# A hybrid attention layer in fp32: other first loads, an order by parts for the first products, two weight splits moved, and the last squares on another engine

## The chip, the cores and the metric

The kernel runs on one core of a Trainium2 chip. The core has five engines with queues of their own: TensorE (PE; its weight loads are listed apart as PEld), VectorE (DVE), ScalarE (ACT), GpSimd (POOL) and SyncE (SP), the last of which only starts transfers here. Engines wait for each other through semaphores; each works through its own queue in order. The time is that of one execution on the device in microseconds, 766.73 as the median of three runs before the change (765.64, 766.73, 766.76).

## The reference

One layer of a trunk on 512 frames of width 1024, with 256 memory tokens, all in float32:

```python
hn = rmsnorm(h, norm_mix_g[l])
proj = hn @ w_in[l]
fq, fk, fv, ff, gq, gf, gi, gg = jnp.split(proj, split_idx, axis=-1)
fox_out = fox_attention(to_heads(fq), to_heads(fk), to_heads(fv), log_f)   # causal softmax, 8 heads of 64
rec = hgrn2_chunkwise(gq, gf, gi, lbs[l])                                  # gated recurrence, 4 heads of 128
rec = rmsnorm(rec, hgrn_norm_g[l]) * silu(gg)
h = h + concatenate([fox_out, rec]) @ w_out[l]
h = h + memory_cross_attention(rmsnorm(h, norm_x_g[l]), rmsnorm(mem, norm_mem_g[l]), w_xq, w_xkv, w_xo)
u = rmsnorm(h, norm_ff_g[l]) @ w1[l]
h = h + square(relu(u)) @ w2[l]                                            # d_ff = 4096
return rmsnorm(h, final_norm_g)
```

The softmax adds to each score the difference of two running sums of log forget gates. The factor of the first RMSNorm depends on the row alone, so the kernel multiplies by it behind the projection.

## The kernel before

**Products.** TensorE computes with operands of a reduced float format (fp32r). Every fp32 operand is split into a high part (a rounding copy) and a low part (what is left), and a product is three: high by high, high by low, low by high. For activations the high part of the normalised x is `hn_hi` and the low part `hn_lo`; for weights they are `wh` and `wl`. `gemm_fm` (L225) runs over the eight chunks of 128 inputs and issues for each chunk the three products L232 (wh by hi), L233 (wh by lo), L234 (wl by hi) of 128x512 elements into one PSUM bank. L245 to L247 are the same for 264 columns.

**Weights.** Panels of 256 columns are loaded on SyncE's queue into raw tiles (`wr`, two halves a and b per panel), and split by `split_of` (L164): ScalarE copies the high part (L167), VectorE subtracts for the low part (L169). `next_panel` (L204) loads and splits one panel ahead of the one in use. Panel 0 comes in quarters (`load_next(4)`), 256 KB each. Panel 11 is the first one of the memory's value projection.

**Order.** TensorE's instructions stand in the order in which the program records them; ScalarE and VectorE are in recorded order only up to the end of the first products. Elsewhere a scheduler sets their order by priorities (`ahead`), and `issue_after` and `keep_in_program_order` bind single instructions. SyncE's queue only starts transfers.

**Stages,** in us of the span: to 23 the loads of x, its transposes (`x_T`, L402, names `xt` and `xn`; four per chunk c) and the first two row blocks of the first panel, products `gf`; to 57 more projections and gates; 57 to 67 the diagonal blocks of the recurrence (`dg`, L611, four heads, 16 products of 64 columns each), with pieces of the projection `gi` between them as fill (`fill.run(F1)`, L614); to 120 the levels of the recurrence; to 150 its state chain; to 270 the softmax attention; to 440 the output projection and the cross attention; then the MLP, and from 755 the last RMSNorm.

**Softmax attention.** 32 units (p, tb, j): head pair, block of 128 queries, head in the pair. For each unit the scores (L881, L882), the mask and maximum on VectorE (L887), the exponential on ScalarE (L889), the scaling (L890, L891), four or fewer transposes into a PSUM slot `pt` (L899) and a copy of these (`ptb`, `pta`; L910 on ScalarE for j = 0, L912 on VectorE for j = 1). Fill runs between: projections `pq` and `pk`, and transposes `mnt` of the memory (L362), whose results are taken by `meh` (ScalarE, L364) and `mel` (VectorE, L365). `mnt` and `pt` share PSUM slots.

**MLP.** Each product of weights by activations is done on 2x2 blocks with seven products instead of eight; an up unit ("u", g, name) multiplies a 512 KB weight block by sums of the input's quarters, a down unit ("d", ...) multiplies by sums of the squared hidden values. `unit` (L1320) prepares splits of coming weight blocks (`prep`, L1308; whu and wlu up, whd and wld down) up to four ahead. Results of up units stand in PSUM banks `uU` and `uY`; `h` (L1398) is a copy held for a later unit, `c` (L1405) adds it, `hb` (L1434, L1436) are the split sums for the down units.

**End.** `squares` (L1513) takes the square of the finished columns on ScalarE with their running sum, adds the sums of the pieces (`fe`, L1521); GpSimd raises them to the power -1/2 (L1544), and both ScalarE and VectorE scale and store the rows.

Of the kernel before, what the change touches and what calls it, by code (L numbers as in the profile page):

```python
# [9 lines left out]
F32 = mybir.dt.float32  # L10
R = mybir.dt.float32r
U8 = mybir.dt.uint8
AF = mybir.ActivationFunctionType
# [29 lines left out]
def emit(  # L43
# [110 lines left out]
    stream = []  # L154
    state = {"used": 0, "then": None}
    UW, UK = WT + FH, KC // 2
# [16 lines left out]
    def load_unit(name, spec, ks, parts=1, between=None):  # L173

        nw = max(sl.stop for sl, _ in spec)
        hi, lo = new_parts([UK, nw], name)
        raw_ = wrp.tile([P, UK * nw], F32, tag="wr", name=f"wr{name}", padded_shape=[P, UK * UW])
        raw_ = raw_.rearrange("p (k n) -> p k n", k=UK)
        nk = UK // parts
        splits = []  # L180
        for q in range(parts):
            qs, src_ks = slice(q * nk, (q + 1) * nk), slice(ks.start + q * nk, ks.start + (q + 1) * nk)
            for sl, src in spec:
                nc.sync.dma_start(raw_[:, qs, sl], src[:, src_ks, :])
            if between is not None:
                between(q)
            splits.append(split_of(hi[:, qs, :], lo[:, qs, :], raw_[:, qs, :]))
        return (hi, lo), splits
# [15 lines left out]
    def next_panel():  # L204
        while len(stream) < min(state["used"] + 2, len(specs)):
            for split in load_next():
                with ahead(PW), ExitStack() as order:
                    for ins in last_copy[-2:] if len(stream) == 10 else ():
                        order.enter_context(tc.issue_after(ins))
                    split()  # L210
        if state["used"] == len(specs) - 1:
            state["then"]()
        r = stream[state["used"]]
        state["used"] += 1
        return r
# [8 lines left out]

    def gemm_fm(ps, wt, col, ahi, alo, n=S, order=range(KC)):  # L225

        whi, wlo = wt
        sl = slice(col, col + P)
        for n_, k in enumerate(order):
            hi, lo = chunk(ahi, k, slice(0, n)), chunk(alo, k, slice(0, n))  # L230
            wh, wl = chunk(whi, k, sl), chunk(wlo, k, sl)
            te.matmul(ps, wh, hi, start=n_ == 0, stop=False)  # L232
            te.matmul(ps, wh, lo, start=False, stop=False)  # L233
            te.matmul(ps, wl, hi, start=False, stop=n_ == KC - 1)  # L234
            yield 3 * n / 2400
# [73 lines left out]
    def load_x(g, n=WT, queue=ac):  # L309
        gs = slice(g, g + n)  # L310
        queue.dma_start(xt[:, :, gs], x[:, gs].rearrange("(t p) n -> p t n", p=P))

    load_x(0, P, nc.sync)
    load_x(P, P)
    for q in range(1, 3):
        load_x(q * WT)
    first = load_next(4)
    load_x(3 * WT, queue=nc.sync)
    rows = t2("rows", F32, (P,))[0:33, :]
# [12 lines left out]
    ve.memset(mhalf, -0.5)  # L332
    ones = cp.tile([P, 1], F32, name="ones")
    ve.memset(ones, 1.0)

# [99 lines left out]
    with tc.manual_schedule(engines={mybir.EngineType.Activation, mybir.EngineType.DVE}):  # L435
# [10 lines left out]
        gfps = [mm(f"gf{i}") for i in range(2)]  # L446
        gfg = [gemm_fm(gfps[i], wt0, i * P, hn_hi, hn_lo) for i in range(2)]
        second = []
# [24 lines left out]
        for c in range(KC):  # L473
            for g in gfg:
                next(g)
# [127 lines left out]
    for hp in range(2):  # L603
        Ac.append(t2(f"Ac{hp}", F32, (8, 64)))
        for j in range(2):
# [7 lines left out]
            gp.tensor_tensor(qt_(h), qt_(h), Fg[hp][:, j, :], op=ALU.mult)  # L613
            fill.run(F1)  # L614

# [247 lines left out]
    units = [(p, tb, j) for p in range(4) for tb in range(NT) for j in range(2)]  # L863
    prob, probT, held_T = {}, {}, {}

# [9 lines left out]
    def fox_scores(u):  # L875
# [7 lines left out]
        with ahead(P3):  # L883
# [4 lines left out]
            den = sm(1, f"dn{h}{tb}")  # L888
            ac.activation(b, b, AF.Exp, bias=mx, scale=-1.0, accum_out=den)  # L889
            ve.reciprocal(den, den)  # L890
            ve.tensor_scalar(b, b, den, None, op0=ALU.mult)  # L891

    def fox_T(u):
# [10 lines left out]
        with ahead(P4):  # L904
            if tb == NT - 1:
                probT[u] = t2(f"pts{h}{tb}")
            else:
                probT[u] = held_T[p, tb % 2][:, j, (0 if tb else 3 * P) :][:, 0:n]
            if j == 0:
                ac.activation(probT[u], pt[:, 0:n], AF.Copy)  # L910
# [26 lines left out]
    for n in range(len(units) + LAG):  # L937
        if n < len(units):
# [19 lines left out]
            if n == 2:  # L958
                fill.until("fv0")
            if n + 1 < len(units):  # L960
                fox_bias(units[n + 1])
# [319 lines left out]

    last_sum = {}

# [24 lines left out]
    def prep(kind, g, name):  # L1308
# [4 lines left out]
        unit_ = new_parts([k, D // k], f"{kind}{g}{name}")  # L1313
        with ahead(PW):
            split_of(unit_[0], unit_[1], raw.rearrange("p (k n) -> p k n", k=k))()
# [4 lines left out]
    def unit(*key):  # L1320
# [4 lines left out]
        kept = sum(k in units and keys.index(k) < keys.index(key) for k in last_keys)  # L1325
        while unit_q and kept + sum(k in units for k in keys[keys.index(key) :]) < 4:
            prep(*unit_q.popleft())
# [100 lines left out]
    def hidden_part(g, name):  # L1428
# [4 lines left out]
        sign = -1.0 if name == "6" else 1.0  # L1433
        ac.activation(hb[:, 0], src, AF.Copy, scale=sign)  # L1434
        if name == "6":
# [77 lines left out]
    def squares(tb, cs, last=False):  # L1513
        n = len(sums.setdefault(tb, []))
        ms = sm(1, f"fm{tb}{n}")
        if tb not in outs:
            outs[tb] = k4([D], f"fo{tb}")
        ac.activation(outs[tb][:, cs], acc[tb][:, cs], AF.Square, scale=1.0 / 32.0, accum_out=ms)
        if n:
            e = sm(1, f"fe{tb}{n}")  # L1520
            (ve if last else gp).tensor_scalar(e, ms, sums[tb][-1], EPS if last else 0.0, op0=ALU.add, op1=ALU.add)  # L1521
            ms = e
# [102 lines left out]
```

## Time and profile before

| What | Value |
|---|---|
| median of three runs | 766.73 us (765.64 to 766.76) |
| profiled execution | 765.97 us, span 763.9 us (2.07 us lie around the span) |
| TensorE busy | 751.6 us (98% of the span) |
| VectorE, ScalarE, GpSimd busy | 559.7, 427.1, 182.9 us |
| waits of TensorE that the profile names | 5.0 us in five places |

The span runs from the first to the last recorded instruction; the run's time is a little longer, and 0.76 us less than the median. A row of the timeline has the start and the duration in us, the engine, the line in the kernel, the operation with output<-input, the shape, and in brackets the idle time of the engine before it with what ended that. A product's recorded duration is longer than its share of the engine, since products overlap; the distance from one start to the next tells what it costs. The profile lists the granted clock of TensorE (PEclk, 1.00 is full).

### The profile page before, as it was taken

To read this page: it belongs to the slowest core of one execution; us is meant where nothing else is said; L and a number is where in the kernel's file an instruction comes from. 1 tells how busy PE (TensorE), PEld (TensorE's weight loads), DVE (VectorE), ACT (ScalarE), POOL (GpSimd) and SP (SyncE) were. 2 spreads that over 40 slices of the span, in tenths; PEclk is the share of its full clock that TensorE was granted. 3 is DMA by queue.
4 is the path that set the end of the run, shared out by engine and by line. 5 is a ranking of instruction groups with operands and counts; after the bars stand their busy time and mean duration, and the time that the engine had idled before them with its cause. 6 is when DMAs were issued, how large, how long until landed. Compare 5 with 4: busy or idle time off the path is not lost.

```text
span 763.9 us, 12648 instructions
## 1 busy us (share of the span) xinstructions
PE 751.6 (98%) x4844; PEld 665.8 (87%) x4844; DVE 559.7 (73%) x889; ACT 427.1 (56%) x718; POOL 182.9 (24%) x261
## 2 busy tenths in 40 slices
PE   8999999999999999999999999999999999999996
PEld 5889878978989988888888898999999999999985
DVE  4746766797677746645557789869797979897984
ACT  4655555676656533334445576656565757565743
POOL 7106343444343005510000111211212121211122
PEclk9999999999999999999999999999999999999998
DMA  7643322243444443221124498896979797978612
GB/s 225 216 114 86 111 82 57 84 111 85 142 161 137 131 150 111 87 79 56 56 83 137 83 295 171 231 253 161 249 165 241 183 268 164 280 148 213 161 47 110
DMA packets 84221, 113.08 MB, mean 148 GB/s; under 512 B 4881, under 2 KB 62778, under 8 KB 84162
## 3 DMA queue, kind: packets, MB, share of 16 engines
q1 hardware_dynamic: 70418, 74.77, 30.9%
q0 software_dynamic: 11568, 35.15, 22.6%
q10 hardware_dynamic: 2176, 2.36, 0.9%
q8 instruction: 38, 0.62, 0.3%
q14 instruction: 21, 0.17, 0.1%
HBM read 88.14 MB, written 4.21 MB: 121 GB/s over the span
## 4 chain that ended last, share of the span: by engine, by line
PE 90%; DVE 3%; DMA 2%; ACT 2%; issue 1%; POOL 1%; POOLq 0%; ACTq 0%; SPq 0%; DVEq 0%
PE uU L1394 4%; PE uU L1393 4%; PE uU L1395 4%; PE U L1495 3%; PE U L1496 3%; PE U L1497 3%; PE uY L1393 3%; PE uY L1395 3%; PE uY L1394 3%; PE xq L232 2%; PE xq L233 2%; PE xw L232 2%; PE xw L234 2%; PE xw L233 2%; PE xq L234 2%; PE wo L233 2%
## 5 line engine op out<-in xcount | busy, mean ns | idle before, releaser
L167 ACT ACTIVATE whd<-wq 128x1024 fp32r<-128x1024 f32 x39 | 41.3, 1058 | 31.3 <-PE U L1497 12.9
L169 DVE TENSOR_TENSOR wld<-wq,whd 128x1024 fp32r<-128x1024 f32 x39 | 47.6, 1220 | 7.1 <-ACT whd L167 7.1
L167 ACT ACTIVATE whu<-uq 128x1024 fp32r<-128x1024 f32 x28 | 29.7, 1062 | 33.0 <-PE uY L1394 14.3
L1395 PE MATMUL uU<-x2s,wlu 128*128 128x256 f32 x160 | 45.3, 283 | 0.0
L1393 PE MATMUL uU<-x2s,whu 128*128 128x256 f32 x160 | 45.2, 283 | 0.0
L1495 PE MATMUL U<-whd,hb 128*128 128x512 f32 x112 | 43.9, 392 | 0.0
L1496 PE MATMUL U<-wld,hb 128*128 128x512 f32 x112 | 43.9, 392 | 0.0
L1497 PE MATMUL U<-whd,hb 128*128 128x512 f32 x112 | 43.6, 389 | 0.0
L1250 POOL DMA_DIRECT2D uk<-us x8 | 7.2, 906 | 149.6 <-ACT acc L1114 85.7
L1467 DVE SCALAR_TENSOR_TENSOR acc<-U,r,acc 128x512 f32<-128x512 f32 x56 | 40.2, 744 | 1.8 <-PE U L1497 1.2
L169 DVE TENSOR_TENSOR wlu<-uq,whu 128x1024 fp32r<-128x1024 f32 x28 | 34.2, 1221 | 5.7 <-ACT whu L167 5.4
L1394 PE MATMUL uU<-x2a,whu 128*128 128x256 f32 x128 | 36.2, 283 | 0.0
L1394 PE MATMUL uY<-x2a,whu 128*128 128x256 f32 x128 | 36.2, 283 | 0.0
L1394 PE MATMUL uU<-x2b,whu 128*128 128x256 f32 x128 | 36.2, 283 | 0.0
L167 ACT ACTIVATE whu<-us 128x1024 fp32r<-128x1024 f32 x20 | 21.2, 1062 | 21.6 <-PE uU L1394 17.9
L169 DVE TENSOR_TENSOR wlu<-us,whu 128x1024 fp32r<-128x1024 f32 x20 | 24.4, 1221 | 10.8 <-ACT whu L167 10.8
L1393 PEld LDWEIGHTS uU<-x2s,whu 128*128 128x128 f32 x160 | 30.6, 191 | 0.8
L1395 PEld LDWEIGHTS uU<-x2s,wlu 128*128 128x128 f32 x160 | 30.6, 191 | 0.0
L889 ACT ACTIVATE bi<-bi,mx 128x128 f32<-128x128 f32 (+3 forms) x32 | 18.0, 561 | 20.5 <-DVE mx L887 20.2
L1250 POOL DMA_DIRECT2D wq<-in_w_dram x10 | 12.2, 1221 | 71.6 <-DMA wq<-in_w_dram 60.9
L872 POOL TENSOR_SCALAR bi<-nF,Ft 128x128 f32<-128x128 f32 (+3 forms) x32 | 21.5, 673 | 31.1 <-PE pt L899 17.1
L1393 PE MATMUL uY<-x2s,whu 128*128 128x256 f32 x96 | 27.3, 284 | 1.0 <-DVE c L1405 1.0
(961 smaller groups left out, 2809.1 us busy)
## 6 DMA issues: line engine op xcount, KB each, us to landing
wq<-in_w_dram SPq DMA_DIRECT2D x31, 512.0 KB, 6.0
uq<-in_w_dram SPq DMA_DIRECT2D x12, 512.0 KB, 4.7
us<-in_w_dram SPq DMA_DIRECT2D x12, 512.0 KB, 6.8
wq<-wq POOLq DMA_DIRECT2D x11, 512.0 KB, 6.4
wq<-in_w_dram POOLq DMA_DIRECT2D x10, 512.0 KB, 9.0
uk<-in_w_dram SPq DMA_DIRECT2D x8, 512.0 KB, 4.1
uk<-us POOLq DMA_DIRECT2D x8, 512.0 KB, 4.5
uq<-uk POOLq DMA_DIRECT2D x8, 512.0 KB, 6.1
```

The lines of the kernel that those rows point to most:

```text
L167: ac.activation(hi, raw, AF.Copy)
L169: ve.tensor_tensor(lo, raw, f(hi), ALU.subtract)
L232: te.matmul(ps, wh, hi, start=n_ == 0, stop=False)
L233: te.matmul(ps, wh, lo, start=False, stop=False)
L234: te.matmul(ps, wl, hi, start=False, stop=n_ == KC - 1)
L1393: te.matmul(ps[:, i, :], whi[:, k, ws], xh, start=first_ and (k, i) == (0, 0), stop=False, skip_group_check=True)
L1394: te.matmul(ps[:, i, :], whi[:, k, ws], xl, start=False, stop=False, skip_group_check=True)
L1395: te.matmul(ps[:, i, :], wlo[:, k, ws], xh, start=False, stop=k == 3, skip_group_check=True)
L1467: ve.scalar_tensor_tensor(a, ps, r2[:, 0 if sign > 0 else 1, tb : tb + 1], a, op0=ALU.mult, op1=ALU.add)
L1495: te.matmul(ps, hi, whi[:, k, :], start=first_ and k == 0, stop=False, skip_group_check=True)
L1496: te.matmul(ps, hi, wlo[:, k, :], start=False, stop=False, skip_group_check=True)
L1497: te.matmul(ps, lo, whi[:, k, :], start=False, stop=k == 1, skip_group_check=True)
```

## The change

Seven edits:

1. x's first three wide pieces no longer go out together on ScalarE's queue, nor the four weight quarters at once on SyncE's: SyncE's queue now has them in turn, x behind w. A copy of a constant into one column of x's tile, on ScalarE, stands before the first wide piece of x, which is held until the copy is done.
2. The six products of the first chunk are ordered by parts (both high by high, both low weight, both low activation) instead of by row block.
3. The fill between the diagonal blocks runs twice as long after each second block, and not at all after each first one.
4. The split of panel 11's second half (wh11b, wl11b) is issued behind the exponential and the scaling of the fourth softmax unit.
5. For the first head pair, all copies of `pt` are on ScalarE.
6. In the MLP, the split of up unit (1, "6") is issued behind the cast hb of unit (0, "6"), and at one step there is room for three prepared units, not four.
7. The squares of the very last 128x256 piece and their sum are one reduction on VectorE that starts from the running sum, and EPS is added one step earlier.

```diff
@@ load_unit
-                nc.sync.dma_start(raw_[:, qs, sl], src[:, src_ks, :])
+                load = nc.sync.dma_start(raw_[:, qs, sl], src[:, src_ks, :])
+                if between is not None:
+                    tc.keep_in_program_order(load)
@@ next_panel
-            for split in load_next():
+            for half, split in enumerate(load_next()):
...
-                    split()
+                    if (len(stream), half) == (12, 1):
+                        later.append(split)
+                    else:
+                        split()
@@ gemm_fm: begun=False added; the chunks' start and stop follow from it and from len(order)
@@ first loads
+    ones = cp.tile([P, 1], F32, name="ones")
+    ve.memset(ones, 1.0)
     load_x(0, P, nc.sync)
     load_x(P, P)
-    for q in range(1, 3):
-        load_x(q * WT)
-    first = load_next(4)
-    load_x(3 * WT, queue=nc.sync)
+    tc.keep_in_program_order(ac.activation(xt[:, 0, WT : WT + 1], ones, AF.Copy))
+
+    def x_behind(part):
+        if part < 3:
+            tc.keep_in_program_order(load_x((part + 1) * WT, queue=nc.sync))
+
+    first = load_next(4, x_behind)
@@ first chunk
-        gfg = [gemm_fm(gfps[i], wt0, i * P, hn_hi, hn_lo) for i in range(2)]
+        for part in ("hh", "lh", "hl"):
+            for i, ps in enumerate(gfps):
+                w, a = (wt0["hl".index(part[0])][0][:, 0, i * P : (i + 1) * P], (hn_hi, hn_lo)["hl".index(part[1])][:, 0, :])
+                te.matmul(ps, w, a, start=part == "hh", stop=False)
+        gfg = [gemm_fm(gfps[i], wt0, i * P, hn_hi, hn_lo, order=range(1, KC), begun=True) for i in range(2)]
@@ diagonal blocks
-            fill.run(F1)
+        fill.run(2 * F1)
@@ fox_scores
-            ac.activation(b, b, AF.Exp, bias=mx, scale=-1.0, accum_out=den)
+            exp = ac.activation(b, b, AF.Exp, bias=mx, scale=-1.0, accum_out=den)
             ve.reciprocal(den, den)
-            ve.tensor_scalar(b, b, den, None, op0=ALU.mult)
+            ends[u] = exp.ins, ve.tensor_scalar(b, b, den, None, op0=ALU.mult).ins
@@ fox_T
-            if j == 0:
+            if j == 0 or p == 0:
@@ the attention's loop
+            if n == 4:
+                with ahead(PW), tc.issue_after(ends[units[3]][0]), tc.issue_after(ends[units[3]][1]):
+                    later.pop()()
@@ prep
-        with ahead(PW):
+        with ahead(PW), tc.issue_after(hb_ins[0, "6"]) if (kind, g, name) == ("u", 1, "6") else nullcontext():
@@ unit
-        while unit_q and kept + sum(k in units for k in keys[keys.index(key) :]) < 4:
+        room = 3 if key == ("u", 1, "2") else 4
+        while unit_q and kept + sum(k in units for k in keys[keys.index(key) :]) < room:
@@ hidden_part
-        ac.activation(hb[:, 0], src, AF.Copy, scale=sign)
+        hb_ins[g, name] = ac.activation(hb[:, 0], src, AF.Copy, scale=sign).ins
@@ squares
+        if last and tb == NT - 1:
+            a = acc[tb][:, cs]
+            tc.keep_in_program_order(ve.tensor_tensor_reduce(out=outs[tb][:, cs], in0=a, in1=a, scale=1.0 / D, scalar=sums[tb][-1], op0=ALU.mult, op1=ALU.add, accum_out=ms))
+            sums[tb].append(ms)
+            return
...
-            (ve if last else gp).tensor_scalar(e, ms, sums[tb][-1], EPS if last else 0.0, op0=ALU.add, op1=ALU.add)
+            (ve if last else gp).tensor_scalar(e, ms, sums[tb][-1], EPS if last or tb == NT - 1 else 0.0, op0=ALU.add, op1=ALU.add)
```

What this does to the order of three queues is shown below; line numbers behind the first edits are higher in the changed kernel.

SyncE's queue at the start of the program, before (`xt` is x's tile, in pieces of 128 or 256 columns; `wr0a` and `wr0b` are panel 0's halves, in quarters; `rows` are small vectors of gains):

```order
L311 DMA xt<-in_x_dram 128x4x128
L184 DMA wr0a<-in_w_in_dram 128x2x256 x2
L184 DMA wr0b<-in_w_in_dram 128x2x256 x2
L311 DMA xt<-in_x_dram 128x4x256
L321 DMA rows<-in_norm_x_g_dram 8x128
```

And with the change:

```order
L316 DMA xt<-in_x_dram 128x4x128
L184 DMA wr0a<-in_w_in_dram 128x2x256
L331 DMA rows<-in_norm_x_g_dram 8x128
L331 DMA rows<-in_norm_mem_g_dram 8x128
L331 DMA rows<-in_norm_ff_g_dram 8x128
L316 DMA xt<-in_x_dram 128x4x256
L184 DMA wr0a<-in_w_in_dram 128x2x256
L316 DMA xt<-in_x_dram 128x4x256
L184 DMA wr0b<-in_w_in_dram 128x2x256
L316 DMA xt<-in_x_dram 128x4x256
L184 DMA wr0b<-in_w_in_dram 128x2x256
```

The two wide pieces of x that were ScalarE's are SyncE's now, each wide piece stands ahead of the weight quarter that is used with it, and three small loads have moved ahead of all of them.

VectorE in the attention, before, around the second unit (L887 is mask and maximum, L890 and L891 the scaling of the first unit, `mel` the low part of the memory's chunk):

```order
L169 TENSOR_TENSOR wl11a<-wr11a,wh11a 128x1024
L890 RECIPROCAL dn_1737<-dn_1737 128x1
L891 TENSOR_SCALAR bi_1661<-bi_1661,dn_1737 128x128
L169 TENSOR_TENSOR wl11b<-wr11b,wh11b 128x1024
L887 ISA bi_1727,mx_1783<-ps_1780,bi_1727 128x128
L887 ISA mx_1783 128x1
L365 SCALAR_TENSOR_TENSOR mel_1791<-mnt_1793,gv,meh_1789 128x256
```

ScalarE with the change, where wh11b now stands (`meh` of two memory chunks, `ptb` the copies of the third and fourth unit, L901 the exponential of the fifth):

```order
L372 ACTIVATE meh_1789<-mnt_1882,gv 128x256
L167 ACTIVATE wh11b<-wr11b 128x1024
L922 ACTIVATE ptb_1893<-pt_1890 128x256
L167 ACTIVATE wh12a<-wr12a 128x1024
L901 ACTIVATE bi_1851,dn_1907<-bi_1851,mx_1905 128x384
L372 ACTIVATE meh_1789<-mnt_1914,gv 128x256
L922 ACTIVATE ptb_1893<-pt_1925 128x256
```

On VectorE, wl11b has left its place behind L891 and stands behind the fifth unit's maximum, directly ahead of wl12a; the last copy above was VectorE's.

ScalarE in the MLP, before (`whu` and `whd` are high parts of up and down weights, `h` the held copy, `hb` the casts of hidden sums `n_0` and `s_0`):

```order
L1434 ACTIVATE hb_4982<-sq_4715 128x512
L167 ACTIVATE whu_5013<-uq_4597 128x1024
L167 ACTIVATE whu_5045<-uq_4596 128x1024
L1434 ACTIVATE hb_5010<-n_0_5007 128x512
L1398 ACTIVATE h_5043<-uU_5018 128x512
L1434 ACTIVATE hb_5101<-s_0_5006 128x512
L167 ACTIVATE whd_5079<-wq 128x1024
```

And with the change:

```order
L1450 ACTIVATE hb_4983<-sq_4716 128x512
L167 ACTIVATE whu_5014<-uq_4598 128x1024
L1414 ACTIVATE h_5044<-uU_5019 128x512
L1450 ACTIVATE hb_5011<-n_0_5008 128x512
L1450 ACTIVATE hb_5102<-s_0_5007 128x512
L167 ACTIVATE whu_5075<-uq_4597 128x1024
L167 ACTIVATE whd_5080<-wq 128x1024
```

The second whu has moved behind h and both casts; h stands ahead of the casts. On VectorE the low part of the same weight moves behind `c` in the same way.

More of the change, by code (lines that the diff above doesn't have):

```diff
@@ L154, in emit @@
     stream = []
-    state = {"used": 0, "then": None}
+    state, later = {"used": 0, "then": None}, []
     UW, UK = WT + FH, KC // 2
@@ L221, in chunk, with gemm_fm @@
         return t[:, k, sl]
-    def gemm_fm(ps, wt, col, ahi, alo, n=S, order=range(KC)):
+    def gemm_fm(ps, wt, col, ahi, alo, n=S, order=range(KC), begun=False):
         whi, wlo = wt
@@ L231, in gemm_fm @@
             wh, wl = chunk(whi, k, sl), chunk(wlo, k, sl)
-            te.matmul(ps, wh, hi, start=n_ == 0, stop=False)
+            te.matmul(ps, wh, hi, start=n_ == 0 and not begun, stop=False)
             te.matmul(ps, wh, lo, start=False, stop=False)
-            te.matmul(ps, wl, hi, start=False, stop=n_ == KC - 1)
+            te.matmul(ps, wl, hi, start=False, stop=n_ == len(order) - 1)
             yield 3 * n / 2400
@@ L310, in load_x @@
         gs = slice(g, g + n)
-        queue.dma_start(xt[:, :, gs], x[:, gs].rearrange("(t p) n -> p t n", p=P))
+        return queue.dma_start(xt[:, :, gs], x[:, gs].rearrange("(t p) n -> p t n", p=P))
+    ones = cp.tile([P, 1], F32, name="ones")
+    ve.memset(ones, 1.0)
     load_x(0, P, nc.sync)
     load_x(P, P)
-    for q in range(1, 3):
-        load_x(q * WT)
-    first = load_next(4)
-    load_x(3 * WT, queue=nc.sync)
+    tc.keep_in_program_order(ac.activation(xt[:, 0, WT : WT + 1], ones, AF.Copy))
[3 more added lines that the diff above has]
+    first = load_next(4, x_behind)
     rows = t2("rows", F32, (P,))[0:33, :]
@@ L332, in emit @@
     ve.memset(mhalf, -0.5)
-    ones = cp.tile([P, 1], F32, name="ones")
-    ve.memset(ones, 1.0)
     def rstd_of(ms, n, name, r=None):
@@ L473, in emit @@
         for c in range(KC):
-            for g in gfg:
+            for g in gfg if c else ():
                 next(g)
@@ L863, in emit @@
     units = [(p, tb, j) for p in range(4) for tb in range(NT) for j in range(2)]
-    prob, probT, held_T = {}, {}, {}
+    prob, probT, held_T, ends = {}, {}, {}, {}
     def fox_bias(u):
@@ L1280, in begin @@
             first_sums(kind, 0)
-    last_sum = {}
+    last_sum, hb_ins = {}, {}
     def behind(kind, g, name):
```

## The prediction

> **What bounds the kernel now.** I read the page's head and busy times first, then TensorE's waits, then the clock and the timeline at each place that the diff touches.
>
> ```profile
> span 763.9 us, 12648 instructions
> ...
> PE 751.6 (98%) x4844; PEld 665.8 (87%) x4844; DVE 559.7 (73%) x889; ACT 427.1 (56%) x718; POOL 182.9 (24%) x261
> ```
>
> TensorE (PE) is busy in 98% of the span; no other engine comes near. A gain can only be time in which PE stands still or is slow, or time behind its last product. The waits of PE say where it stands still (us in total, times, longest):
>
> ```profile
> PE xn L405 <- DMA xt<-in_x_dram: 1.8, 1, 1.8
> PE warm L330 <- DVE zero L327: 1.3, 1, 1.3
> PE uY L1393 <- DVE c L1405: 1.0, 1, 1.0
> PE pt L899 <- DVE mel L365: 0.5, 1, 0.5
> PE mnt L362 <- DVE ptb L912: 0.4, 1, 0.4
> ```
>
> These five lines are 5.0 us. The warm-up's 1.3 is the start of the program, which the diff leaves alone; the other four, 3.7 us, lie where the diff works: the first loads, one MLP step, two places in the softmax attention. A wait shows only stopped time. Slow time shows in the granted clock, here of two stretches (columns: length, busy us of PE, PEld, DVE, ACT, POOL, then PEclk, DMA share, GB/s):
>
> ```profile
> 5.10:8.50 3.40, 1.61 (x10) 1.06 (x9) 1.35 (x2) 1.88 (x3) 3.40 (x10) 1.00 1.07 370
> 8.50:11.90 3.40, 3.40 (x11) 2.54 (x10) 0.99 (x2) 0.97 (x3) 3.40 (x14) 0.50 0.92 322
> ```
>
> PE was busy 1.61 of 3.40 us while it waited for x; in the next 3.40 us it was busy all the time, at half clock. Half of 3.40 us, 1.7 us, is lost there without any wait.
>
> **The first loads (and the order of the first six products).** Before, x's later quarters go out on ScalarE's queue beside the weights on SyncE's, so all of them share the bandwidth from the first microsecond; now x and w alternate on SyncE's queue, and the first wide load of x is held behind a one-column copy on ScalarE.
>
> ```profile
> 1.45 1.53 ACTq L311 DMA_DIRECT2D xt<-in_x_dram  x3
> ...
> 3.01 1.28 ACT L167 ACT_TABLE_LOAD   x1 [3.01 <-issue]
> ...
> 5.86 0.63 ACT L167 ACTIVATE wh0a<-wr0a 128x512 fp32r<-128x512 f32 x1 [1.57 <-DMA wr0a<-in_w_in_dram]
> ...
> 6.39 0.67 ACT L408 ACTIVATE hn_hi<-xn,g_mix 128x512 fp32r<-128x512 f32 x1
> ...
> 7.13 0.74 DVE L411 SCALAR_TENSOR_TENSOR hn_lo<-xn,g_mix,hn_hi 128x512 fp32r<-128x512 f32 x1
> 7.13 0.66 PE L405 MATMUL xn<-ident,xt 128*128 128x128 f32 x4 [1.79 <-DMA xt<-in_x_dram]
> ...
> 12.66 0.60 PE L405 MATMUL xn<-ident,xt 128*128 128x128 f32 x4
> ...
> 13.33 0.39 PE L233 MATMUL gf<-hn_lo,wh0a 128*128 128x512 f32 x1
> ...
> 13.56 0.40 PE L234 MATMUL gf<-hn_hi,wl0a 128*128 128x512 f32 x1
> ```
>
> ```profile
> GB/s 0 0 0 0 0 63 130 238 279 246 206 230 315 344 350 350 350 379 386 372 389 363 369 383 377 395 380 383 386 386 386 345 145 59 47 18 0 0 4 3
> ...
> xt<-in_x_dram SPq DMA_DIRECT2D x1, 256.0 KB, 3.1
> ```
>
> The GB/s line cuts 0 to 14 us into 40 slices of 0.35 us; summed, the first 786 kB (x's first two pieces and the first weight quarter) are through after about 5.1 us, and 1310 kB after about 6.6. Before, those bytes were shared with loads that nobody wanted yet, so the first quarter's split began at 5.86 and x's second piece let PE go at 7.13. Now they are asked for almost alone. I estimate: split 5.15 to 5.78 (0.63), the high part of the first chunk until 6.45 (0.67), and there the first product, since the new order asks only for the two high parts. The low weight is ready by then; the low activation takes 0.74 more, to 7.2, and is asked for last. Six products at 0.23 apart (13.33 to 13.56) end near 7.8. The next x quarter is there (6.6 plus an allowance of 0.6 for its completion), four transposes take 0.35, six more products 1.4: the transposes that stood at 12.66 stand at about 9.7. That is 2.95 us, in which the 1.7 us of half clock is included. If the half clock stays, 1.3 is left. I take 2.6, near the upper end, because the work between 5.1 and 8.5 would be about 0.5 (transposes) and 2.05 (6.45 to 8.5), 2.55 of 3.40 instead of 1.61; I shade it for loads that come a little later. After 12.66 PE waits nowhere until the MLP apart from the two attention waits, so what is won here should be kept. ScalarE loses two DMA issues (two thirds of 1.53, 1.0 us), so its table load moves to about 2.0 and the hold-back copy lies at 3.3 to 3.45; behind it on ScalarE is only the first split, which waits for its load anyway. SyncE gains two issues, all before the loads they start are wanted.
>
> **The diagonal blocks.** Four groups of 16 small products each stood between pieces of the fill; now two groups stand together, twice.
>
> ```profile
> 59.94 0.69 PE L611 MATMUL dg<-sta,mov 128*64 128x64 f32 x16
> 60.56 0.39 PE L245 MATMUL gi<-wh4b,hn_hi 128*128 128x264 f32 x1
> 60.78 0.29 PE L246 MATMUL gi<-wl4b,hn_hi 128*128 128x264 f32 x1
> 60.91 0.29 PE L247 MATMUL gi<-wh4b,hn_lo 128*128 128x264 f32 x1
> ```
>
> The first fill product behind a group holds PE for 0.22 us, its successor for 0.13: 0.09 for the way back, and I put the way in at about the same. Two round trips disappear: 2 x 0.18, 0.4 us (0.2 to 0.6, since the way in is not measured alone). VectorE and GpSimd get both results later by at most one fill piece; nothing in the waits of PE is released by them.
>
> **The attention.** The second half of a weight's split (wl11b on VectorE, wh11b on ScalarE) moves behind the fourth softmax, and four copies go from VectorE to ScalarE.
>
> ```profile
> 156.39 1.38 DVE L169 TENSOR_TENSOR wl11b<-wr11b,wh11b 128x1024 fp32r<-128x1024 f32 x1
> ...
> 158.43 0.33 PE L899 MATMUL pt<-ident,bi 128*128 128x128 f32 x1 [0.54 <-DVE mel L365]
> ```
>
> ```profile
> 165.42 1.06 ACT L167 ACTIVATE wh12a<-wr12a 128x1024 fp32r<-128x1024 f32 x1 [0.36 <-PE pk L233]
> ...
> 167.08 0.45 ACT L364 ACTIVATE meh<-mnt,gv 128x256 fp32r<-128x256 f32 x1
> ...
> 167.73 0.40 DVE L912 COPY ptb<-pt 128x256 f32<-128x256 f32 x1
> ...
> 168.19 0.44 PE L362 MATMUL mnt<-ident,mt 128*128 128x128 f32 x2 [0.40 <-DVE ptb L912]
> ```
>
> The 1.38 us split stands ahead of the subtraction (mel) whose end PE waits for; with it gone, the 0.54 goes. The second wait, 0.40, is for a copy that stands on VectorE now and on ScalarE after the change, behind meh, which ends at 167.53: if nothing else moved, the copy would run from 167.55 to 167.95 instead of 167.73 to 168.13, 0.2 sooner. But wh11b (1.06, the size of wh12a) joins the same stretch of ScalarE ahead of wh12a, which had only 0.36 of idle in front of it, so the chain can run 0.7 late and the copy end at 168.65, 0.5 later than before. So the two places together bring 0.54 + 0.2 = 0.7 at best and 0 if the whole 0.7 reaches PE; I take 0.4, the middle, since the rows don't show how much of ScalarE's idle time further up is left. On VectorE, wl11b now stands directly ahead of wl12a, with four copies less around it, and PE asks for neither before the projection in hand is done.
>
> **The MLP step.**
>
> ```profile
> 466.32 1.06 ACT L167 ACTIVATE whu<-uq 128x1024 fp32r<-128x1024 f32 x1 [4.20 <-DMA uq<-uk]
> ...
> 467.81 0.58 ACT L1398 ACTIVATE h<-uU 128x512 f32<-128x512 f32 x1
> ...
> 468.54 1.22 DVE L169 TENSOR_TENSOR wlu<-uq,whu 128x1024 fp32r<-128x1024 f32 x1
> ...
> 469.68 0.68 DVE L1405 TENSOR_TENSOR c<-uY,h 128x512 f32<-128x512 f32 x1
> ...
> 470.42 0.39 PE L1393 MATMUL uY<-x2s,whu 128*128 128x256 f32 x1 [0.95 <-DVE c L1405]
> ```
>
> ScalarE stood 4.20 us in front of a load, and h, which was ready to be copied, stood behind it; VectorE then ran the split before c. Now that split comes after the two casts hb: h and c are done long before 469.4, where PE wants the bank. Gain 0.95, I write 1.0 as in the waits. What is late next is the split itself: h ended at 468.39; one more cast of like length, then 1.06 and 1.22 put its end near 471.3, and it is wanted one unit of 24 products of 0.12 us after 469.4, at 472.3. A margin of 1 us, so 0 to 1.0.
>
> **The last squares.**
>
> ```profile
> 757.23 0.42 ACT L1518 ACTIVATE fo<-acc 128x256 f32<-128x256 f32 x1 [0.86 <-DVE acc L1467]
> ...
> 758.14 0.99 POOL L1544 TENSOR_TENSOR fr<-fe,mhalf 128x1 f32<-128x1 f32 x1 [0.89 <-DVE fe L1521]
> ```
>
> ```profile
> 159.40 0.41 DVE L887 CUSTOM_DVE_ANT_0 bi<-ps,bi 128x256 f32<-128x256 f32 x1
> ```
>
> From the square's start, released by the last acc, to the power on GpSimd it takes 0.91: the square on ScalarE, a read of its sum, an addition on VectorE, two hand-overs between engines. One reduction on VectorE takes their place; the nearest row, of the same size, is 0.41, and I add 0.2 for the read of its sum and the one hand-over that is left: about 0.6. Gain 0.3 (0.2 to 0.4).
>
> **The sum.** 2.6 + 0.4 + 0.4 + 1.0 + 0.3 = 4.7 us. The profiled execution took 765.97 (its span 763.9 and 2.07 around it), so 761.27; it is 0.76 below the median of the runs, 766.73, against which the change is timed, so 762.0.
>
> **Rivals.** *The half clock stays* (20%): the front brings 1.3 instead of 2.6, total 763.3. For it: PE still has a pause of over 0.5 us before 6.45, and the record does not show where the threshold lies between 1.61 of 3.40 and full. Against it: in the record the clock was full right behind a busy stretch. [...]
>
> *The attention's wait moves to ScalarE's queue* (8%): all of wh11b's 1.06 reaches the copy and PE's second wait grows by 0.86 (1.06 less the 0.2); the term falls from +0.4 to 0.54 - 0.86 = -0.3, total 762.7. That wh12a had only 0.36 of idle ahead of it speaks for this; against it, that 0.36 at least is there to take it.
>
> *The alternation does nothing* (7%): the bytes come in the order they came in, the front stays where it was, total 764.6. The 370 GB/s in the first stretch speaks for it (the rate is the limit, not the order); but the order of the bytes is exactly what changes.
>
> *Slower: the loads drain one after the other* (5%). With one queue a load might only start to flow when its predecessor has landed. Rows of loads with little beside them:
>
> ```profile
> wr1a<-in_w_in_dram SPq DMA_DIRECT2D x1, 512.0 KB, 3.7
> ```
>
> ```profile
> 20.31 0.48 PE L232 MATMUL gf<-hn_hi,wh0b 128*128 128x512 f32 x1
> ```
>
> By 3.7 us for 512 KB and 3.1 for 256 KB, starting at 3.45: x 7.2, w 10.3, x 14.0, w 17.1, x 20.8, w 23.9. The product that needs the last quarter, at 20.31 before, would come at 24.55 (0.65 for the split): 4.24 lost, 2.1 won elsewhere: 766.73 + 4.24 - 2.1 = 768.9. It decides once that last quarter lands after about 21.8, where the loss eats the 2.1. Against it: the rate of 350 to 390 in the GB/s line was held by both queues together, but a queue whose next load is already issued should not run dry.
>
> **How the numbers follow.** The forecast has 60%. A difference under 0.2%, 1.5 us, can't be told from no change here: faster means below 765.2, slower above 768.3. The forecast and the first two rivals are faster but for their tails, the third mostly, the last is slower or same: 0.87, 0.08, 0.05. The forecast's own range is 760.0 to 763.2 (all upper bounds together, 2.95 + 0.6 + 0.7 + 1.0 + 0.4 = 5.65, would give 761.1, and the runs of before lie 1.1 apart, 765.64 to 766.76, so 1.1 below that; above, the front at 1.9 and the attention at 0 cost 1.1). With the rivals that are faster it is 760.0 to 764.9; what is left out is the slow rival and part of the third.
>
> **What would show it.** Right: the clock row for 8.5 to 11.9 at 1.00; the transposes of 12.66 at 9.5 to 10.2; the wait of PE for x under 1 us; no uY wait; the pt wait gone; the power on GpSimd about 0.6 behind the start of the last reduction. Wrong: half clock anywhere after 5; PE waiting for wh0b or for x's last quarter near 14 to 20; a new wait of mnt or pt for ScalarE at 165 to 169; PE waiting for the MLP split at 472. PE standing still anywhere else would be a cause that this sum lacks.

## The result, and the profile after

The changed kernel takes 760.83 us in the median of four runs (760.0 to 762.03), beside 766.18 for the kernel before in its own four (765.36 to 766.76). The ratio is 0.9932, with a 95% interval of 0.9914 to 0.995: 3.8 to 6.6 us faster. In a later comparison on one chip (five runs beside nine of before) the ratio was 0.9948, 0.9935 to 0.996. The forecast was 762.0, with 760.0 to 764.9. The number was right; how it came about was right in part only.

The head of the page of the changed kernel, and TensorE's waits (us in total, times, longest):

```profile
span 758.8 us, 12648 instructions
...
PE 749.2 (99%) x4844; PEld 664.3 (88%) x4844; DVE 559.3 (74%) x886; ACT 427.7 (56%) x721; POOL 185.4 (24%) x261
```

```profile
PE warm L340 <- DVE zero L337: 1.3, 1, 1.3
PE xn L413 <- DMA xt<-in_x_dram: 0.7, 1, 0.7
```

The span is 5.1 us shorter. All three waits behind the front (uY, pt, mnt) are gone from the list, and the wait for x has gone from 1.8 to 0.7. The clock of the two stretches that the prediction looked at (columns as there):

```profile
5.10:8.50 3.40, 2.65 (x13) 1.85 (x14) 2.11 (x3) 1.86 (x3) 3.40 (x10) 1.00 0.94 300
8.50:11.90 3.40, 3.40 (x19) 2.58 (x18) 1.97 (x3) 2.47 (x5) 3.40 (x11) 1.00 1.03 362
```

In this execution the half clock from 8.5 to 11.9 is gone. To see where the time went I put each TensorE product of this trace beside the same product of the trace before and took the difference of their starts. A step in that difference is a place where time was won or lost. From the timeline of the changed kernel, the products at the steps and what they depend on:

```profile
5.72 0.66 PE L413 MATMUL xn<-ident,xt 128*128 128x128 f32 x4 [0.68 <-DMA xt<-in_x_dram]
...
6.33 0.74 PE L458 MATMUL gf<-hn_hi,wh0a 128*128 128x512 f32 x2
...
10.00 0.60 PE L413 MATMUL xn<-ident,xt 128*128 128x128 f32 x4
...
54.87 0.69 PE L623 MATMUL dg<-mov,sta 128*64 128x64 f32 x16
55.38 0.64 PE L623 MATMUL dg<-sta,mov 128*64 128x64 f32 x16
55.95 0.39 PE L250 MATMUL gi<-wh4a,hn_hi 128*128 128x264 f32 x1
```

```profile
154.58 0.27 PE L911 MATMUL pt<-ident,bi 128*128 128x128 f32 x1
...
163.11 0.47 ACT L372 ACTIVATE meh<-mnt,gv 128x256 fp32r<-128x256 f32 x1
...
163.61 0.38 ACT L922 ACTIVATE ptb<-pt 128x256 f32<-128x256 f32 x1
164.05 0.44 PE L370 MATMUL mnt<-ident,mt 128*128 128x128 f32 x2
```

```profile
451.29 0.19 PEld L1409 LDWEIGHTS uU<-x2s,whu 128*128 128x128 f32 x1 [0.30 <-DVE c L1421]
...
460.09 0.60 ACT L1414 ACTIVATE h<-uU 128x512 f32<-128x512 f32 x1 [1.75 <-PE uU L1411]
...
464.32 0.68 DVE L1421 TENSOR_TENSOR c<-uY,h 128x512 f32<-128x512 f32 x1
...
465.52 0.28 PE L1409 MATMUL uY<-x2s,whu 128*128 128x256 f32 x1
```

The transposes that stood at 12.66 stand at 10.00 (9.7 was forecast). Two diagonal groups are 0.51 apart. The first pt stands without a wait at 154.58, 3.85 before its old 158.43. One new stop of 0.30 has come at 451.29, where TensorE waits for VectorE's c. And h runs at 460.09, so that c ends at 465.00 and uY follows at 465.52 at once.

The table gives this difference for all profiles, in us earlier than in the profile of before, at the end of each part: the front (the same product at 16 us before), the diagonal blocks (66), the attention (171), a point ahead of the MLP step (460), behind it (471), and the last products (756). The last column says when, after 5.5 us, TensorE ran at half pace, by the distances of starts (products of 128x512 elements 0.43 us apart in place of 0.23, transposes of x 0.21 in place of 0.11): "until" where the pace had been half from the start, two times where it went back from full to half.

| Kernel | 16 | 66 | 171 | 460 | 471 | 756 | half pace after 5.5 us |
|---|---|---|---|---|---|---|---|
| before | 0 | 0 | 0 | 0 | 0 | 0 | 8.5 to 11.9 |
| whole change, first profile | 2.44 | 3.13 | 4.14 | 3.78 | 5.00 | 4.99 | none |
| whole change, e10 | 2.40 | 3.08 | 4.09 | 4.08 | 5.29 | 5.32 | until 6.5 |
| front alone, e1 | 2.87 | 2.86 | 2.82 | 2.84 | 2.58 | 2.58 | none |
| all but the front, e2 | 1.61 | 2.25 | 3.25 | 3.24 | 4.46 | 4.48 | none |
| all but the front, e11 | 0.39 | 1.06 | 2.06 | 2.06 | 3.28 | 2.84 | until 9.8 |
| no hold, e3 | 0.79 | 1.48 | 2.48 | 2.47 | 3.69 | 3.71 | 7.5 to 10.9 |
| old six, e4 | 0.77 | 1.46 | 2.47 | 2.52 | 3.74 | 3.61 | until 9.3 |
| old six, e12 | 2.16 | 2.84 | 3.84 | 3.85 | 5.07 | 5.09 | none |
| before with cover, e5 | 1.64 | 1.60 | 1.59 | 1.59 | 1.14 | 1.14 | none |
| weight back, e6 | 2.46 | 3.15 | 3.46 | 3.46 | 4.68 | 4.67 | none |
| copies back, e7 | 2.64 | 3.33 | 2.40 | 2.37 | 3.59 | 3.58 | until 6.8 |
| with two more edits, e9 | 2.54 | 3.21 | 4.20 | 4.19 | 5.41 | 5.10 | none |
| with two more edits, e13 | 0.85 | 1.52 | 2.53 | 2.52 | 3.74 | 3.73 | until 10.1 |

### The profile page after: what moved, and what is told of

The parts are those of the page before. It is cut to its first block, busy times and chain, and to the rows that moved or that the text cites. A ratio compares the mean times of both kernels' runs of the same rounds, so it can differ in the third digit from the quotient of the medians.

```text
span 758.8 us, 12648 instructions
## 1 busy us (share of the span) xinstructions
PE 749.2 (99%) x4844; PEld 664.3 (88%) x4844; DVE 559.3 (74%) x886; ACT 427.7 (56%) x721; POOL 185.4 (24%) x261
## 4 chain that ended last, share of the span: by engine, by line
PE 96%; DMA 2%; DVE 1%; ACT 0%; issue 0%; POOL 0%; POOLq 0%; ACTq 0%; SPq 0%; DVEq 0%
PE uU L1409 4%; PE uU L1410 4%; PE uU L1411 4%; PE U L1511 3%; PE U L1512 3%; PE U L1513 3%; PE uY L1411 3%; PE uY L1410 3%; PE uY L1409 3%; PE xq L237 2%; PE xq L238 2%; PE xw L239 2%; PE xq L239 2%; PE xw L237 2%; PE xw L238 2%; PE wo L237 2%
## 5 line engine op out<-in xcount | busy, mean ns | idle before, releaser
L884 POOL TENSOR_SCALAR bi<-nF,Ft 128x128 f32<-128x128 f32 (+3 forms) x32 | 23.2, 728 | 29.9 <-PE pt L911 16.6
L901 ACT ACTIVATE bi<-bi,mx 128x128 f32<-128x128 f32 (+3 forms) x32 | 18.0, 561 | 19.2 <-DVE mx L899 18.8
```

## The experiments

**The front alone, and everything but the front.** e1 is the kernel before with the first two edits; e2 and e11 are the whole change without them.

```diff
# e2, e11, against the changed kernel
-    tc.keep_in_program_order(ac.activation(xt[:, 0, WT : WT + 1], ones, AF.Copy))
-    first = load_next(4, x_behind)
+    for q in range(1, 3):
+        load_x(q * WT)
+    first = load_next(4)
+    load_x(3 * WT, queue=nc.sync)
...
-        for part in ("hh", "lh", "hl"):
...
+        gfg = [gemm_fm(gfps[i], wt0, i * P, hn_hi, hn_lo) for i in range(2)]
```

> The kernel before with the first two edits alone (loads in turn and held back, first six products by parts). Theory: the front is worth 2.4 us by the alignment of the two traces (the transposes of 12.66 stand at 10.00 after the whole change, and the gain is 2.44 from 16 us on), and nothing behind depends on it: 766.2 - 2.4 = 763.8, clock row of 8.5 to 11.9 at 1.00, all of the later waits (pt 0.5, mnt 0.4, uY 1.0) unchanged. Rival: being early only moves the waits to later weight loads, and part of it is given back before the MLP ends: 764.5 to 766.

Measured: 763.55 (763.1 to 763.92), ratio 0.997, interval 0.9959 to 0.9982, so 1.4 to 3.1 us faster. The lead of 2.87 at 16 us is kept to 460, and 0.26 of it is lost in the MLP step that was not changed here. Its waits and the rows there:

```profile
PE uY L1402 <- DVE c L1414: 1.2, 1, 1.2
...
PE pt L908 <- DVE mel L370: 0.6, 1, 0.6
PE mnt L367 <- DVE ptb L921: 0.4, 1, 0.4
```

```profile
463.73 1.06 ACT L167 ACTIVATE whu<-uq 128x1024 fp32r<-128x1024 f32 x1 [4.45 <-DMA uq<-uk]
```

The wait for c grew from 1.0 to 1.2, and ScalarE stood 4.45 in front of the load instead of 4.20: that step hangs on a transfer which does not come earlier by as much as TensorE does (the split behind it starts at 463.73 instead of 466.32, 2.59 earlier, beside the lead of 2.84). So the old order in the MLP gives back part of what is won ahead of it (0.45 in e5). That the MLP edit takes the step off this transfer is a benefit that the forecast did not name.

> The whole change without the first two edits. Theory: the diagonal blocks 0.70, the attention 1.0, the MLP step 1.2, the end 0.17: 3.1 in all, 763.1; the 0.36 that the whole change lost near 455 us (a product uU that waits for c on VectorE, behind a quadrant sum that waits 1.74 us for a weight load) came from TensorE being 4.1 us ahead of its loads there, and is absent at a lead of 1.7. Rival: that loss belongs to the MLP edit itself or to the loads' own scatter and stays: 2.7 in all.

Measured: 761.07 (760.77 to 761.81), ratio 0.9939, interval 0.9926 to 0.9951: 3.8 to 5.7 us faster, without any edit of the front. By the table the parts are 0.64 for the diagonal blocks (0.69 in most of the others), 1.00 for the attention, 1.22 for the MLP step, 0.02 of scatter. The stop near 451 isn't there. But its front, which is the old one, stands 1.61 earlier than in the profile of before. The waits for x with the old loads, in e2 and then in e11:

```profile
PE xn L408 <- DMA xt<-in_x_dram: 0.3, 1, 0.3
```

```profile
PE xn L408 <- DMA xt<-in_x_dram: 1.3, 1, 1.3
```

They are 0.3 and 1.3 where the profile of before has 1.8: x's second piece let TensorE go at 5.74 and 6.73 instead of 7.13. So the profile of before was an execution with a front that was slow even for the old loads, and the 2.44 of the first pair compares unlike executions. The 3.1 that was expected by the starts lies below this interval and inside that of e11 (2.5 to 4.4 us, below); why e2 is faster than its parts is open.

**The hold-back.** e3 leaves the copy out, and so the wait of the first wide piece of x.

```diff
-    tc.keep_in_program_order(ac.activation(xt[:, 0, WT : WT + 1], ones, AF.Copy))
```

> The whole change without the one-column copy that holds the first wide piece of x back; x and w still alternate on SyncE's queue, the small row loads fall behind them. Theory: the order on one queue does most, but the wide piece now shares the bandwidth with x's second small piece: that lands up to 0.7 us later than 5.7, and the front loses 0.3 to 0.7. Rival: the hold is what makes the front, since without it the wide piece flows from 2 us on as before: the transposes of 10.0 are back at 11 or later, with half clock. Second rival: the hold does nothing (within 0.1).

Measured: 761.18 (760.24 to 762.08), ratio 0.9935 (0.992 to 0.995). In its profile x's second piece let TensorE go at 6.33 instead of 5.72, 0.6 later, where the theory gave up to 0.7. TensorE waited 1.4 for it, and at 7.5 the pace went back from full to half until 10.9; the transposes stood at 11.85. Here the clock rows show it, as they do in the profile of before:

```profile
5.10:8.50 3.40, 2.17 (x9) 1.71 (x10) 2.17 (x3) 1.89 (x3) 3.40 (x10) 0.85 1.04 279
8.50:11.90 3.40, 3.40 (x14) 2.68 (x13) 0.90 (x2) 1.21 (x2) 3.40 (x10) 0.64 1.08 381
```

These are the only two profiles of the fourteen with a return to half, and the two with the longest waits for x (1.8 and 1.4; e11, with 1.3, was still at the half pace of the start). Its runs lie at 760.24 and 760.38, and at 761.98 and 762.08, so the hold is not decisive in each execution: half of these have the time of the whole change without it. By this one profile the hold brings x's second piece 0.6 sooner (in the nine profiles with the hold these transposes start between 5.39 and 5.98); no difference of the time is shown.

**The pause of TensorE covered.** e5 is the kernel before with eight products on zeros in the pause from 5.3 to 7.1; they add work that no result uses.

```diff
         x_T(0)
+        cover = pvt("cover")
+        for _ in range(8):
+            te.matmul(cover, zero[:, 0:P], zero, start=True, stop=True)
         x_T(1)
```

> The kernel before with eight products on zeros between the first and the second transposes of x, so that TensorE does not stand still from 5.3 to 7.1; loads as before. They change no result. Theory: the half clock of 8.5 to 11.9 is the consequence of that pause; it is gone, and the products behind 8.5 come 1.7 us sooner at 12.66 as long as the loads let them: between 0.8 and 1.7 us faster. Rival: the half clock does not come from the pause (it stays at the same place): no change, or a loss of up to 0.3 where the zeros delay the transposes.

Measured: 765.6 (764.51 to 766.63, eleven runs) beside 765.4 (sixteen runs), ratio 0.9999, interval 0.999 to 1.0008. No gain. Its profile has no half pace, but neither has e2's, with the same loads and no cover. So covering the pause does not pay on the average, and my reading that the pause in the profile of before cost each execution 1.7 us falls. Of 27 other executions of the kernel before, in two comparisons, two show a granted clock as low as that profile's 0.995; the rest have 0.997 or more, and so have all nine of the last comparison. A return to half for 3.41 us would lower this figure by 0.002 (half of 3.41 in 763.9), so it is rare; that a long pause brings it about where it comes is not refuted by e5, and e3 speaks for it.

**The order of the first six products.** e4 and e12 have the old order (both are the changed kernel with the lower half of the diff of e2).

> The whole change with the first chunk's six products in the old order, row block by row block. Theory: the second product waits for the low activation (ready near 7.1 in the profile of the whole change) instead of running at 6.7 beside it; the six end 0.3 to 0.5 us later, and the transposes of 10.00 stand at 10.3 to 10.5. Rival: the next x quarter decides there anyway and nothing moves (within 0.1).

> The whole change with the old order of the first six products, now timed. Its first profile lost 1.7 us at 16 us, in an execution whose products stood 0.43 us apart until 9.1 (half pace) and 0.23 apart behind. Theory: that was the execution, not the order; the order is worth 0.2 to 0.5 us. Rival: it is worth 1 us or more in every execution, because the first products' wait keeps TensorE at half pace longer.

e4 ran once, with the profile (762.04 us), and lost 1.7 us at 16 us, far more than the 0.3 to 0.5 of the theory; e12 lost 0.24 to 0.28 against the whole change. Timed, e12 has 761.85 (760.65 to 761.96), ratio 0.995 (0.9937 to 0.9962), beside 0.9948 for the whole in the same comparison. The order is worth about 0.25 by this one profile, which is inside the scatter of the others (the new loads and order at full pace stand between 2.40 and 2.87 at 16 us) and is not resolved by the times. The rest of e4's loss is half pace. Its products and its clock row:

```profile
7.78 0.63 PE L239 MATMUL gf<-hn_hi,wl0a 128*128 128x512 f32 x1
8.21 0.63 PE L237 MATMUL gf<-hn_hi,wh0a 128*128 128x512 f32 x1
8.64 0.63 PE L238 MATMUL gf<-hn_lo,wh0a 128*128 128x512 f32 x1
```

```profile
5.10:8.50 3.40, 3.06 (x10) 2.15 (x9) 2.10 (x3) 1.89 (x3) 3.40 (x10) 1.00 0.96 259
```

The products start 0.43 apart, nearly twice the 0.23 of full pace, while the column PEclk says 1.00. In the second profile of the whole change the same kind of products stand like this:

```profile
9.07 0.40 PE L239 MATMUL gf<-hn_hi,wl0a 128*128 128x512 f32 x1
9.31 0.40 PE L237 MATMUL gf<-hn_hi,wh0a 128*128 128x512 f32 x1
9.54 0.39 PE L238 MATMUL gf<-hn_lo,wh0a 128*128 128x512 f32 x1
```

So for the start of the program the distance of the products is the evidence for the clock, and the clock row is not: in these traces the clock record begins with the first change to full (at 5.11 us in the profile of before, 4.49 in that of the changed kernel, 9.3 in e4), and the column counts the time ahead of it as full (1.00 from 1.7 to 5.1 us in the profiles of before and of the changed kernel, with the warm-up's products 0.43 apart). How long the start stays at half pace differs between executions of one kernel: until about 9.3 us in e4, and not at all behind 6.4 in e12.

**The attention, each half undone.** e6 puts the weight's split back, e7 the copies.

```diff
# e6
-                    if (len(stream), half) == (12, 1):
+                    if False:
...
-            if n == 4:
-                with ahead(PW), tc.issue_after(ends[units[3]][0]), tc.issue_after(ends[units[3]][1]):
-                    later.pop()()
# e7
-            if j == 0 or p == 0:
+            if j == 0:
```

> The whole change with the split of wl11b and wh11b at its old place. Theory: the stop of TensorE ahead of the first pt is back, 0.7 to 0.8 us in the alignment of the traces, and the second place (mnt behind ptb) gains or loses under 0.3. Rival: with the copies on ScalarE, VectorE has room enough and the stop is under 0.3.

> The whole change with the first pair's copies for j = 1 on VectorE again. Theory: the four copies are worth 0.2 to 0.4 us together, since VectorE now has wl11b and wl12a back to back near 162 us and the copy of the fourth unit would stand behind them: a stop ahead of mnt there of 0.5 to 1.5 us. Rival: no difference (within 0.1): only the weight mattered.

Each ran once, with the profile (760.96 and 762.09 us), so these readings go by the starts alone. e6: the wait at the first pt is back, and the attention brings 0.31 instead of 1.00. Of the 0.77 that the step at pt is worth, 0.02 are left; at the second place 0.29 are won. e7: much worse than expected. The step at pt is won, but 1.9 us are lost behind it, so that the attention brings 0.93 less than nothing. The reason in its waits and its timeline:

```profile
PE mnt L370 <- DVE ptb L924: 1.7, 1, 1.7
```

```profile
162.09 1.25 DVE L169 TENSOR_TENSOR wl11b<-wr11b,wh11b 128x1024 fp32r<-128x1024 f32 x1
...
163.26 1.21 DVE L169 TENSOR_TENSOR wl12a<-wr12a,wh12a 128x1024 fp32r<-128x1024 f32 x1
...
165.26 0.41 DVE L924 COPY ptb<-pt 128x256 f32<-128x256 f32 x1
...
165.82 0.41 PE L370 MATMUL mnt<-ident,mt 128*128 128x128 f32 x2 [1.68 <-DVE ptb L924]
```

The two splits stand back to back on VectorE from 162.09 to 164.47, and the copy that was ready at about 163.8 waits for both, a softmax step and a scaling. The two edits are one: moving the weight without moving the copies would have cost 0.93 in place of winning 1.00.

**The whole again, and two more edits.** e10 is the changed kernel. e9 and e13 add that the second row block's squares ahead of the MLP's sums go to ScalarE, and the addition ahead of the last reduction to VectorE.

```diff
-        if tb == 0:
+        if tb < 2:
             square = ac.activation(junk, acc[tb], AF.Square, scale=1.0 / 32.0, accum_out=ms2[:, tb : tb + 1])
...
-            (ve if last else gp).tensor_scalar(e, ms, sums[tb][-1], ...
+            (ve if last or tb == NT - 1 else gp).tensor_scalar(e, ms, sums[tb][-1], ...
```

> The whole change, with two more edits: the squares of the second row block ahead of the MLP's first sums go from VectorE to ScalarE (so that c does not stand behind a 1.22 us reduction), and the addition ahead of the very last reduction goes from GpSimd (busy with a power of 1.0 us until 0.3 us before) to VectorE. Theory: the 0.36 us near 451 us is gone and the end is 0.1 to 0.2 us shorter, 0.5 us in all: 760.3 beside 760.8. Rival: c is late because of the load that the quadrant sum waits for, not because of the reduction, and the stop moves to the next product: no change.

> The whole change again, beside the next three on the same chip. The front is worth 2.4 us by the first pair of profiles, but the profiled execution of before was one of the few with half clock from 8.5 to 11.9 (granted clock 0.995; 25 of 27 others have 0.997 or more), and two profiles with the old loads and full clock stand 1.6 us earlier at 16 us. Theory now: against ordinary executions the front is worth 0.8 to 1.0 us, so the whole is about 0.9 us below the rest without the front, 4.9 to 5.2 below the kernel before. Rival: the front is worth its 2.4 and the whole stands 2 us or more below the rest. Second rival: the front is worth nothing once the rest is there.

> The whole change without the first two edits, again, for the difference to the whole: theory 0.9 us slower than the whole, rival 2 us or more, second rival equal.

> The whole change with the second row block's squares on ScalarE and the addition ahead of the last reduction on VectorE, again, for the difference to the whole. Theory: 0.3 us faster than the whole (the end 0.27, near 451 us 0.41, of which 0.34 is lost again at 544 us behind a copy on ScalarE). Rival: no difference.

e9 had 760.39 (759.58 to 762.62), ratio 0.9934 (0.9911 to 0.9957). In the last comparison, all on one chip beside the same runs of before: e10, the whole, 761.91 (760.35 to 762.0), ratio 0.9948; e11, all but the front, 761.83 (761.0 to 762.71), ratio 0.9954 (0.9942 to 0.9967); e13 761.74 (760.0 to 761.93), ratio 0.9943 (0.993 to 0.9957). The difference that the front makes on top of the rest is not resolved by the times; the rival of a full 2 us falls, that of nothing does not. Beside e1's 1.4 to 3.1 us for the front alone, on another chip, its size stays open. The two more edits are no faster by the times either. The stop near 451 is not in e10, the same kernel with the same lead (4.08), so it is scatter of the loads (in the first profile VectorE's sum uq waited 1.74 us for one at 446.53) and not a price of being early, as I had it; e9 lost 0.34 at another place, 544 us, where ScalarE stood 4.43 us in front of a load and h behind it, and e11 lost there too.

The runs of the whole change lie in two groups: 760.0, 760.35, 760.37, 760.8 and 760.85, and 761.91, 761.94, 762.0 and 762.03. Of the profiled executions with the new loads, the three with half pace as late as 9.3 us (e3, e4, e13) took 761.74 to 762.08, and the five at full pace from 6.5 us on (first profile, e6, e9, e10, e12) 760.35 to 760.96; e7 is the odd one, with its own 1.9. That the two groups are the two paces is what this suggests; it is shown for the profiled executions alone.

## Why the prediction was right or wrong

**The front (forecast 2.6): the mechanism of the new loads right, the size wrong against an ordinary execution.** The split began at 5.07 (5.15 forecast), the first product stood at 6.33 (6.45), the transposes at 10.00 (9.7). The 0.3 at the end are the allowance for the next x quarter: the sum had it at 7.2, of which 0.6 for the completion was my estimate and stood in no row, and it let TensorE go at 8.13, where the six products would have ended near 7.8. The busy time of 5.1 to 8.5 was 2.65 (2.55 forecast), and the clock stayed full. (Of x's three wide pieces, two were on ScalarE's queue before; the third was SyncE's already, behind the weights.)

The step that failed is the other side of the difference. The term took the late second piece of x (7.13), the pause of 1.8 and the 1.7 us of half clock behind it for what every execution of the kernel before pays. With the same loads, e2 and e11 had that piece at 5.74 and 6.73 and neither went back to half. Like with like, the table gives: at full pace 2.40 to 2.87 against 1.61 and 1.64, so 0.8 to 1.3; with half pace until about 10 us 0.85 (e13) against 0.39 (e11), so 0.5. The rival "the half clock stays" (20%) did not come as it was told: no profile with the complete new front went back from full to half. But half pace from the start lasted until 10.1 in e13, with that front, and the forecast had no term for this. No run shows the threshold of busy time of which that rival speaks; there was a return to half behind 1.62 and 1.96 busy us of 3.41, and none behind 2.59 or more.

**The diagonal blocks (0.4, bounds 0.2 to 0.6): too low.** 0.69, in every profile with the edit between 0.64 and 0.69. The way out and the way in are what I priced; missing was the group's own tail: 16 products take 0.62 from their start to the next product when fill follows (59.94 to 60.56) and 0.51 when another group follows (54.87 to 55.38). The second group of a pair takes 0.57 (55.38 to 55.95), 0.05 less than alone. With 0.18 for the round trip (0.09 measured for the way back, 0.09 my estimate for the way in) that is 0.34 for each of two places.

**The attention (0.4, bounds 0 to 0.7): too low, outside the bounds.** 1.00. The wait of 0.54 was worth 0.77 by the starts: the idle time counts only from the recorded end of the product ahead of the stop (0.40 behind its start, where the next product would stand 0.23 behind it), and the first two products behind the stop also ran apart. Two smaller steps between the places, 0.18 won and 0.24 lost, nearly cancel; their causes are open. The second place won 0.2 to 0.3 where I allowed for a loss: meh ended at 163.58, 3.95 before its old 167.53, so ScalarE's chain ran 0.2 late against TensorE's 4.1 and not 0.7, and the copy followed at 163.61.

**The MLP step (1.0, 0 to 1.0): right in its cause, 1.22 in size, outside the bounds.** Here too the wait of 0.95 understates the stop: the product ahead of it started at 469.07, and 0.23 behind that, at 469.30, the next could have stood, 1.12 before 470.42; the first products behind the stop start 0.22 apart and not 0.12, which is the other 0.10. The split that would be late next was on time.

**The end (0.3): 0.17.** I left out what the new reduction starts from:

```profile
752.06 0.30 POOL L1542 TENSOR_SCALAR fe<-fm,fm 128x1 f32<-128x1 f32 x1
...
752.40 0.49 DVE L1536 CUSTOM_DVE_ANT_0 fo<-acc,fe 128x256 f32<-128x256 f32 x1 [0.19 <-POOL fe L1542]
...
752.98 1.00 POOL L1565 TENSOR_TENSOR fr<-fm,mhalf 128x1 f32<-128x1 f32 x1 [0.61 <-DVE fm L1536]
```

The running sum fe comes from GpSimd, which was still in the power of the row block before; the reduction waits 0.19 for it. From the reduction's start to the power it took 0.58, as forecast (0.6). With that addition on VectorE (e9 and e13) the reduction does not wait, and the end brings 0.33 and 0.34.

**The sum.** 2.44 + 0.69 + 1.0 + 1.22 + 0.17 less 0.36 of scatter at 451 make the 5.1 of the first pair of profiles. Forecast were 4.7, from a front that was too large by 1.3 to 2.1 against ordinary executions and other terms that were too small by 1.0 together. Against ordinary executions the parts add up to 3.6 to 4.4 (the front 0.5 to 1.3, then 0.69, 1.0, 1.22 and 0.17), beside the 4.0 of the last comparison (0.9948 of 765.25; 3.1 to 5.0 by its interval) and the 5.2 of the first. So the total was met by luck: errors of both signs cancelled. The slow rival, loads that drain one after the other, found nothing: wh0b's product of 20.31 stood at 17.88, 2.43 us earlier, and 300 and 362 GB/s moved in the two stretches from 5.1 to 11.9, with the wide loads on SyncE's queue alone.

## What to carry to other kernels

A term read from one profiled execution needs a second one: what differs from execution to execution (here the landing of x's second piece, and the pace of the first 12 us) looks like a property of the kernel. Measure each edit alone and all but that edit; the difference of starts, product by product, then gives terms of a few tenths that no timing resolves. A wait in the list was less than its stop (0.54 against 0.77, 0.95 against 1.22), since the products around it run apart too, and a move that clears one engine's queue must be costed with what now stands behind it, as e7 shows.

## What the runs showed of the hardware that I had not expected

Half pace in the front has two forms. The first is the start. In all fourteen profiles the first six products, the warm-up, start 0.43 us apart from 1.7 us on; eight of the same shape in e5 stand 0.22 apart later. This half pace ends at a time that differs from execution to execution, of one kernel too: by 5.7 us in nine profiles, near 6.5 in e10, 6.8 in e7, 9.3 in e4, 9.8 in e11 and 10.1 in e13. e4 and e12, one kernel, are 1.4 us apart at 16 us. The column PEclk says 1.00 over this time.

The second is a return from full to half, in two profiles, and the clock record has it: 8.52 to 11.94 in the profile of before, 7.51 to 10.92 in e3. Ahead of it the record has full pace for 3.41 us (from 5.11 and from 4.10), in which TensorE was busy for 1.62 and 1.96. In the other twelve it was busy for 2.59 (e12) to 3.41 of the first 3.41 us at full pace, and the clock stayed full. Between 1.96 and 2.59 nothing was measured. The end of the start does not follow the busy time alone: e3 came to full pace at 4.10 behind 2.74 of 3.42 us, and e13 was at half pace behind 3.07 of 3.41 (3.26 to 6.67). I counted these stretches from the recorded changes; that the busy time of such a stretch is what sets the clock, no run here shows.
